# Attention of a hybrid decoder layer: keys requested ahead of the last group norm, the last head four slots later, value buffers laid over the keys; feed-forward: second half of the norm, splits and residual loads in another order

## The chip, the core and the metric

The kernel runs on one core of one Trainium2 chip. The metric is device time in microseconds (us), the median of several executions. TensorE (PE in the profile) multiplies matrices, VectorE (DVE) and ScalarE (ACT) work on elements, GpSimd (POOL) does little here, and SyncE (SP) issues most transfers. Each engine executes its own instructions in the order written for it, and waits on semaphores for the others.

## The reference

One layer of a decoder is computed for a prompt of 1024 tokens and for 8 sample tokens, 1032 columns in all. All data are float32.

```python
xn = rmsnorm(x, w)                                  # the same for the three mixers
sc_b, sc_c, sc_x, z, xbc, dt, q, gates = split(xn @ w_in)
y_a = (sc_b * conv3(sc_c * sc_x)) @ w_sc_out        # gated short convolution
y_b = group_rmsnorm(ssd(conv4(xbc), dt) * silu(z)) @ w_ssm_out   # Mamba-2, 32 heads, 4 groups
probs = softmax(q @ mem_k * 256 ** -0.5)            # 4 heads of 256, 256 memory tokens
y_c = (probs @ mem_v) @ w_attn_o
g_a, g_b, g_c = split(sigmoid(gates))
x = x + (g_a * y_a + g_b * y_b + g_c * y_c) @ w_merge_o
x = x + (silu(rmsnorm(x) @ w_gate) * (rmsnorm(x) @ w_up)) @ w_down   # hidden width 2816
y = rmsnorm(x)
```

The prompt's keys and values come from its memory tokens; each of the 8 sample rows has cached keys and values of its own. The outputs also hold new convolution and recurrent states.

## The kernel before

Activations lie transposed: 128 channels of a block on the partitions, 1032 tokens along the free axis. Every float32 operand of a matmul is split into a high and a low half (a copy on ScalarE, a subtraction on VectorE), and a product is made of three matmuls: high by high, high by low, low by high. In the names, a last `h` or `l` is a half, `r` a raw load.

`gemm` (L200) makes 128 rows of an output from 8 blocks of input, 3 halves and 512 + 256 + 264 columns, so 72 matmuls. Between the blocks it calls `tick()`, which runs the next piece of the list `pend`. The side work stands in that list: scan pieces during the input projections, attention pieces during the second output projection. `pace` is the length of the list over the number of matrices left, so the pieces are spread evenly, and a piece that is moved or removed shifts those behind it.

The stages in the order of time: norm and input projections; the scan's pieces between the gate products and the first output projection (`wo00` to `wo07`); the second output projection, whose 16 blocks of input come in two halves (`wo10` to `wo17`, `wo20` to `wo27`), with the attention pieces between its matmuls; `wo30` to `wo37` for the attention's output; the merge (`pm`, L1855) with the sum of squares for the second norm; the feed-forward part, whose products go by one level of Strassen's scheme; the final norm.

The attention pieces (list `pieces`, L1717): load the prompt's keys `kk` (`k_load`, L1553, onto SP), turn them on TensorE (`k_turn`, `pskT`, L1567) and split them into `kTh`, `kTl` (L1569, L1570); load a head's queries `qT` (`a_load`, L1665) and split them into `q00h` and so on; scores per 256 tokens (`a_scores`, `psa`, L1679), softmax (L1597 to L1606, `mx`, `pr`), turned probabilities (`a_probs`, `psp`, `pTh`, `pTl`), products with the values (`a_out`, `psv`, L1711). Beside them run the sample's rows `b` from 0 to 7: broadcast query `qb` (one buffer), cached keys `kc` (two buffers), scores on VectorE (L1588), and in the end one softmax and per row `s_values` (loads `vc`, in the buffers of `kc`) and `s_out` (`pso`, L1638, sixteen matmuls, eight for each half of the memory). Score tiles share two PSUM buffers. While `wo17` runs, the eight blocks of the second half are loaded (`in`, L1443, onto SP) and split into `b00` to `b07`.

In the last scan group, `group_norm` writes its four normed blocks to `yb_d` (L1198, onto SP). The keys and queries stand behind these on SP's queue.

The feed-forward part: `st_early` (L272) makes the first half of six products while the second half of the norm is not there yet; `norm_half` (psf L1804, psr L1817) makes the inverse root from the sums of squares `sq` (L1867) and spreads it. `strassen` (L311) makes four outputs out of seven products of 24 matmuls, called `B11`, `T1`, `nT2`, `B21`, `T3`, `B22`, `T4` after their right operand, on three PSUM tiles `m0` to `m2`. `first` evacuates a product (L319); in the down projection, `d00` to `d16`, it adds to the residual `x` in place (`into`). `used` runs a refill: after a product has used a right operand, the splits for the next half of the hidden blocks (`h0T30l` and so on, L1961). `tc.issue_after(i)` makes the scheduler place what follows behind instruction i on its engine. `residual` loads `x` again (L2004); `product` finishes the last hidden pair (L1980 to L1982).

Of the kernel before, what the change touches and what calls it, by code (L numbers as in the profile page):

```python
# [9 lines left out]
F32 = mybir.dt.float32  # L10
F32R = mybir.dt.float32r
# [6 lines left out]
P = 128  # L18
# [29 lines left out]
def tile_kernel(ctx: ExitStack, tc, a, o):  # L48
# [185 lines left out]
    pst = [None]  # L234
    freed = [None]
    count = [0]

# [33 lines left out]

    def st_early(blocks, forms):  # L272


        for first in range(0, len(blocks), 3):
            held = []
            for i, (src1, nm, out, keep) in enumerate(blocks[first : first + 3]):
                wA = st_split(st_raw(src1, f"{nm}Er"), f"{nm}E")
                ps = st_ps(f"m{i}", f"{nm}e")
                o1 = out()  # L280
                st_prod(forms, ps, wA, 0, "B11", True)
                S.copy(o1[:, HS[1]], hv(ps))
                held.append((wA, ps, o1, keep))
            for wA, ps, o1, keep in held:
                st_prod(forms, ps, wA, 512, "B21", False)
                S.copy(o1[:, HS[0]], hv(ps))
                keep(o1)
# [23 lines left out]
    def strassen(  # L311
# [5 lines left out]
        def first(dst, ps):  # L317
            if into:
                V.tensor_tensor(dst, ps, dst, op=ALU.add)  # L319
            else:  # L320
                S.copy(dst, ps)

        def used(f):
            turning.append(refill(f) if refill is not None else None)
            if len(turning) > LATE:
                g = turning.popleft()
                if g is not None:
                    g()

# [46 lines left out]
        if early is None:  # L376
            first(o12, hv(pa))
            used("nT2")
            prod(pc, wA, 512, "B21", True)
            V.tensor_tensor(o11, hv(pc), o11, op=ALU.add)  # L380
            used("B21")
        else:
            S.copy(o21, o12)
            V.tensor_sub(o22, o22, o12)
            freed[0] = V.tensor_tensor(o12, hv(pa), o12, op=ALU.add).ins
        if ready is None:
# [1110 lines left out]
    for i, (src, w) in enumerate(ins[:3]):  # L1497
# [5 lines left out]
            for m in range(KD)  # L1503
        )
    for g in range(GROUPS):
        xg, bcg, hold = groups[g]
# [5 lines left out]
        pend.extend(pieces[-3:])  # L1512
        pend.extend(z_pieces(g, xg, hold) + [None] + group_norm(g, xg, hold))
    pace[:] = len(pend) / (len(fillers) + KD) + 1e-6, 0.0
# [28 lines left out]
    if True:  # L1543
        kTh = at.tile([P, KD, MEM], F32R, tag="kTh", bufs=1, name="kTh")
        kTl = at.tile([P, KD, MEM], F32R, tag="kTl", bufs=1, name="kTl")
        vh = at.tile([P, 2, D], F32R, tag="vh", bufs=1, name="vh")
        vl = at.tile([P, 2, D], F32R, tag="vl", bufs=1, name="vl")
        sc_s = tri[:, 64:].rearrange("p (m b h) -> p m b h", m=2, b=NS)
        pTs = qs.rearrange("p t b -> p (t b)").rearrange("p (m c) -> p m c", m=2)

        kks = {}

        def k_load(m):  # L1553
            kks[m] = ev_tile(f"kk{m}", (P, D))
            SY.dma_start(kks[m], k_d[m])

# [70 lines left out]

        def s_values(b):
            for m in range(2):
                kcs[b, m] = at.tile([P, D], F32, tag="kc", name=f"vc{b}{m}")  # L1630
                SY.dma_start(kcs[b, m], a["cache_mem_v"][0, b, m * P : (m + 1) * P].rearrange("m h d -> m (h d)"))

        def s_out(b):
# [9 lines left out]
            S.copy(t, ps[:, :256])  # L1643
            if b + 1 < NS:
                s_values(b + 1)
            for h in range(AH):
# [56 lines left out]
        def a_out(h, dk):  # L1703
# [13 lines left out]
        pieces = [  # L1717
            [(k_load, 0), (k_load, 1), (a_load, 0)],
            [(k_turn, 0, 0)],
# [3 lines left out]
        for h in range(AH):  # L1723
# [3 lines left out]
            if h + 1 < AH:  # L1727
                pieces.append([(a_load, h + 1)])
            pieces.append([(a_out, h, 0)])
            pieces.append([(a_out, h, 1)])  # L1730
            if h == 2:
                pieces.extend([] for _ in range(4))
        pieces[5].append((k_turn, 1, 1))
        pieces[6].append((v_in, 1))
        for b in range(NS):
            at_ = 3 + 5 * b
            for i, fs in enumerate(
# [8 lines left out]
        pieces = [lambda fs=fs: run(fs) for fs in pieces]  # L1746
        pieces += [s_softmax, lambda: s_values(0), s_probs, None]
        for b in range(NS):
            pieces += [lambda b=b: s_out(b), None]
        pend.extend(pieces)  # L1750
        pend.extend(states)
        pend.extend([None, s_back])
        pace[:] = len(pend) / (len(outs) - 1) + 1e-6, 0.0
# [88 lines left out]
    for half in range(2):  # L1842
# [30 lines left out]
        else:  # L1873
            flush()
            norm_half(1, sq)
    aux_stack.close()
# [14 lines left out]
    for i, (nm, j) in enumerate((("g", 0), ("u", 0), ("g", 2), ("u", 2), ("g", 4), ("u", 4))):  # L1891
# [10 lines left out]
        )  # L1902
    st_early(blocks, forms)
    for kt in range(4):
# [100 lines left out]

    residual(0, 1, 2, 3)

    def opening():
        product()
        residual(4, 5, 6, 7)  # L2010

    for ch in range(2):
        for m in range(0, KD, 2):
# [3 lines left out]
                lambda m=m: (x2[m][:, HS[0]], x2[m][:, HS[1]], x2[m + 1][:, HS[0]], x2[m + 1][:, HS[1]]),  # L2017
                into=True, hook=opening if ch == 0 and m == 0 else None, **turn,
            )
# [134 lines left out]
```

## Time and profile before

| | us |
|---|---|
| median of 3 executions | 2461.08 (2458.73 to 2466.34) |
| the profiled execution | 2456.66 |
| its span, first to last instruction | 2454.6 |
| TensorE busy | 2425.3 (99%) |
| VectorE busy | 1582.8 (64%) |
| ScalarE busy | 1065.7 (43%) |
| mean granted TensorE clock | 0.997 |

A row of the waits names the waiting engine and the line, what ended the wait, the time in total, how often and the longest. A row of the timeline gives start, duration, engine, line, operation, output and inputs, and in brackets the idle time before it and what ended it; several alike are joined (x3). A row of the stretches gives from and to, the length, busy time by engine, the granted clock (1.00 is full speed), the share of the transfer engines and GB/s. [...]

### The profile page before, as it was taken

How to read it: one execution, taken by the hardware profiler on the slowest of the kernel's cores; microseconds unless marked ns; L12 is line 12 of the kernel's file. 1: busy time of each engine (PE TensorE's matmuls, PEld its weight loads, DVE VectorE, ACT ScalarE, POOL GpSimd, SP SyncE). 2: the span in 40 equal slices, each digit the busy share in tenths (PEclk: the TensorE clock that was granted, in tenths of full speed). 3: DMA queues.
4: the chain of work that ended last, by engine and by line, in shares of the span. 5: the costliest groups of instructions: out<-in, count | busy, mean ns of one | idle time of the engine just before them, and what ended most of it. 6: DMA issues, size and time to landing. Idle time of an engine off the chain costs nothing.

```text
span 2454.6 us, 45661 instructions
## 1 busy us (share of the span) xinstructions
PE 2425.3 (99%) x18946; PEld 2309.6 (94%) x18946; DVE 1582.8 (64%) x2591; ACT 1065.7 (43%) x1707; POOL 121.0 (5%) x163
## 2 busy tenths in 40 slices
PE   9999999999999999999999999999999999999998
PEld 7999999999999999888888887899999999999998
DVE  6854677777676774657767662555787555476756
ACT  6554455453545536456445441223443333342322
POOL 0200000000000001121120000000000000000000
PEclk9999999999999999999999999999999999999999
DMA  6445344354344456667867686865443323264421
GB/s 199 134 127 172 120 131 130 107 158 117 112 122 146 138 151 217 200 203 258 273 215 274 212 286 228 297 198 168 147 161 130 113 82 115 76 234 137 149 86 70
DMA packets 358622, 404.35 MB, mean 165 GB/s; under 512 B 16406, under 2 KB 285830, under 8 KB 358407
## 3 DMA queue, kind: packets, MB, share of 16 engines
q1 hardware_dynamic: 337966, 343.72, 44.9%
q10 hardware_dynamic: 20449, 57.71, 6.1%
q8 instruction: 149, 2.44, 0.4%
q14 instruction: 58, 0.48, 0.1%
HBM read 286.31 MB, written 115.29 MB: 164 GB/s over the span
## 4 chain that ended last, share of the span: by engine, by line
PE 88%; DVE 5%; DMA 4%; ACT 2%; issue 1%; SPq 0%; POOL 0%; ACTq 0%; DVEq 0%
PE po L220 13%; PE ps_q L220 4%; PE pm L1855 3%; PE ps_g L220 2%; PE pd L220 1%; PE py L1058 1%; PE pss L1071 1%; PE ps_z L220 1%; PE po L1050 1%; PE Z6m L266 1%; PE Z2m L266 1%; PE Z8m L266 1%; PE C3m L266 1%; PE Z14m L266 1%; PE C6m L266 1%
## 5 line engine op out<-in xcount | busy, mean ns | idle before, releaser
L1003 ACT ACTIVATE r<-r,acum 128x128 f32<-128x128 f32 x256 | 79.2, 392 | 4.6 <-DMA r<-ac_d 4.2
L774 DVE SCALAR_TENSOR_TENSOR ax<-u,prm,ax 128x1024 f32<-128x1024 f32 x44 | 56.4, 1281 | 0.3 <-ACT ax L771 0.2
L1035 POOL TENSOR_TENSOR xdd<-xdt,decst 128x512 f32<-128x512 f32 x32 | 37.0, 1157 | 293.1 <-DVE xdt L1031 293.1
L944 ACT ACTIVATE st<-st,es 128x128 f32<-128x128 f32 x128 | 41.5, 392 | 23.0 <-DMA st<-in_state_ssm_dram 17.6
L1054 DVE TENSOR_TENSOR y<-po,ea 128x512 f32<-128x512 f32 x28 | 19.3, 690 | 39.9 <-PE po L1050 37.1
L1490 DVE TENSOR_TENSOR yr<-po,yr 128x1032 f32<-128x1032 f32 x8 | 9.9, 1232 | 54.4 <-PE po L220 53.7
L946 DVE SCALAR_TENSOR_TENSOR st<-sr,dts,st 128x128 f32<-128x128 f32 x128 | 40.9, 354 | 0.4
L1029 DVE TENSOR_TENSOR r<-r,cbm 128x1024 f32<-128x1024 f32 x32 | 39.2, 1225 | 2.8 <-ACT bT L1028 0.5
L950 DVE SCALAR_TENSOR_TENSOR sr<-st,sr 128x128 f32<-128x128 f32 x128 | 36.1, 293 | 1.1
L1028 ACT COPY bT<-bp 128x128 f32<-128x128 f32 x32 | 8.5, 264 | 64.9 <-DVE cbm L1026 64.8
L2089 ACT ACTIVATE fj<-psy 128x512 f32<-128x512 f32 (+1 forms) x18 | 10.7, 596 | 58.3 <-PE psy L2087 58.2
L1071 PE MATMUL pss<-xdd,bT 128*128 128x512 f32 x64 | 33.4, 604 | 2.5 <-ACT bT L1028 2.5
L1058 PE MATMUL py<-r,xdt 128*64 128x128 f32 x512 | 35.0, 279 | 0.0
L1004 ACT ACTIVATE r<-r 128x1024 f32<-128x1024 f32 x32 | 33.8, 1058 | 0.7
L1031 DVE TENSOR_TENSOR xdt<-xp,dtT 128x512 f32<-128x512 f32 x32 | 21.9, 686 | 18.7 <-PE xp L1024 18.5
L1862 DVE TENSOR_TENSOR x<-pm,xT 128x516 f32<-128x516 f32 x16 | 11.1, 696 | 35.1 <-PE pm L1855 35.1
L1084 POOL TENSOR_TENSOR s<-s,cdec 128x512 f32<-128x512 f32 x28 | 32.0, 1143 | 4.8 <-DVE s L1077 4.5
L1058 PEld LDWEIGHTS py<-r,xdt 128*64 128x64 f32 x512 | 27.3, 136 | 4.2 <-issue 0.5
L1050 PE MATMUL po<-bc,s 128*128 128x128 f32 x224 | 29.8, 276 | 0.0
L1784 DVE TENSOR_TENSOR gt<-po,gt 128x1032 f32<-128x1032 f32 x8 | 9.9, 1232 | 29.8 <-PE po L220 29.2
L1588 DVE SCALAR_TENSOR_TENSOR kc<-kc,qb 128x256 f32<-128x256 f32 x64 | 23.5, 421 | 7.9 <-DMA qb<-qs_d 7.1
L777 DVE SCALAR_TENSOR_TENSOR ax<-u,prm,ax 128x1032 f32<-128x1032 f32 x22 | 28.4, 1290 | 0.0
(9065 smaller groups left out, 9063.0 us busy)
## 6 DMA issues: line engine op xcount, KB each, us to landing
r<-ac_d SPq DMA_DIRECT2D x32, 512.0 KB
gt<-gt_d SPq DMA_DIRECT2D x24, 516.0 KB
xs_d<-ax ACTq DMA_DIRECT2D x22, 516.0 KB
gt_d<-G ACTq DMA_DIRECT2D x20, 516.0 KB
x<-xs_d SPq DMA_DIRECT2D x16, 516.0 KB
zs<-zs_d SPq DMA_DIRECT2D x16, 516.0 KB
yb_d<-x SPq DMA_DIRECT2D x16, 516.0 KB
in<-yb_d SPq DMA_DIRECT2D x16, 516.0 KB
```

Of the source, the lines that this page charges most:

```text
L220: PE.matmul(out[:, c : c + n], wt[:, ks], x[:, c : c + n], start=(k == 0 and i == 0), stop=(k == nk - 1 and i == 2),)
L266: PE.matmul(hv(ps)[:, c : c + n], wt[:, ks], x[:, c : c + n], start=(start and kt == 0 and i == 0), stop=(kt == 3 and i == 2), skip_group_ ...
L774: V.scalar_tensor_tensor(acc[:, :T], u[:, j : j + T], w[j], acc[:, :T], op0=ALU.mult, op1=ALU.add)
L944: S.activation(st[:, i], st[:, i], AF.Copy, scale=es[:, g * 4 + i, b : b + 1])
L946: V.scalar_tensor_tensor(st[:, i], rb, dts[:, g * 4 + i, b : b + 1], st[:, i], op0=ALU.mult, op1=ALU.add)
L1003: S.activation(r[:, j, :], r[:, j, :], AF.Relu, scale=-1.0, bias=acum[:, c, h : h + 1])
L1029: V.tensor_tensor(r, r, bc(cbm.unsqueeze(1), [P, HPG, P]), op=ALU.mult)
L1035: G.tensor_tensor(b3(xdd, HPG), b3(xdt, HPG), bc(decst[:, c, hs].unsqueeze(2), [P, HPG, 64]), op=ALU.mult)
L1050: PE.matmul(po[:, t * P : (t + 1) * P], state["s"][:, t * P : (t + 1) * P], bcg[1][:, cs], start=True, stop=True,)
L1058: PE.matmul(py[hp : hp + 64, (h // 2) * P : (h // 2 + 1) * P], xdt[:, h * 64 : (h + 1) * 64], r[:, (h % 2) * 4 + h // 2, :], start=True, s ...
L1071: PE.matmul(pss, bT, xdd, start=True, stop=True)
L1855: PE.matmul(hv(ps)[:, c : c + n], wt[:, ks], x[:, half * HT + c : half * HT + c + n], start=(k == 0 and i == 0), stop=(k == KD - 1 and i = ...
```

## The change

1. The two key loads leave the first attention piece. They become a piece of their own just ahead of the last group's `group_norm`, and use activation buffers (tags `ah`, `al`) instead of `ev` buffers.
2. `kTh` and `kTl` get a pool of their own, which is closed at the second row of values. A pool of four value buffers is opened over it. Rows 0, 3 and 6 use the two old buffers, the others the four new ones. `s_out(b)` requests the values of row b + 3 instead of b + 1.
3. Behind head 2 stand eight slots instead of four, with the last conv state, the sample's softmax and its turned probabilities in them. The other conv states go along with `a_load`; before, all four stood at the end of the list. The sample's rows follow each other every four pieces instead of five. The list has 71 entries instead of 73, so the pace goes from 4.87 to 4.73 pieces a matrix.
4. `norm_half(1, sq)` moves from ahead of the early products to behind the first of them.
5. In `strassen`, the refill's splits are placed behind the last splits of weights and behind the last evacuation (`out[0]`).
6. The residual loads: blocks 0 and 1 first, 2 and 3 with `product`, 4 to 7 with the second pair of outputs. Before, 0 to 3 first and 4 to 7 with `product`.

```diff
+    out = [None]
...
-    def st_early(blocks, forms):
+    def st_early(blocks, forms, then):
...
                 st_prod(forms, ps, wA, 0, "B11", True)
                 S.copy(o1[:, HS[1]], hv(ps))
                 held.append((wA, ps, o1, keep))
+                if first + i == 0:
+                    then()
...
             if into:
-                V.tensor_tensor(dst, ps, dst, op=ALU.add)
+                out[0] = V.tensor_tensor(dst, ps, dst, op=ALU.add).ins
...
                 if g is not None:
-                    g()
+                    with tc.issue_after(prev["hi"]), tc.issue_after(prev["lo"]), tc.issue_after(out[0]):
+                        g()
...
-            freed[0] = V.tensor_tensor(o12, hv(pa), o12, op=ALU.add).ins
+            freed[0] = out[0] = V.tensor_tensor(o12, hv(pa), o12, op=ALU.add).ins
...
+    def k_load(m):
+        kks[m] = act_tile(("ah", "al")[m], f"kk{m}", F32)[:, :D]
+        SY.dma_start(kks[m], k_d[m])
...
-        pend.extend(z_pieces(g, xg, hold) + [None] + group_norm(g, xg, hold))
+        pend.extend(z_pieces(g, xg, hold) + [None])
+        if g == GROUPS - 1:
+            pend.append(lambda: [k_load(m) for m in range(2)])
+        pend.extend(group_norm(g, xg, hold))
...
-        kTh = at.tile([P, KD, MEM], F32R, tag="kTh", bufs=1, name="kTh")
-        kTl = at.tile([P, KD, MEM], F32R, tag="kTl", bufs=1, name="kTl")
...
+        akt = ExitStack()
+        keys = akt.enter_context(tc.tile_pool(name="akt", bufs=1, reuse_waits="tile"))
+        kTh = keys.tile([P, KD, MEM], F32R, tag="kTh", name="kTh")
+        kTl = keys.tile([P, KD, MEM], F32R, tag="kTl", name="kTl")
+        vcp = []
...
         def s_values(b):
+            if b == 1:
+                akt.close()
+                vcp.append(att_stack.enter_context(tc.tile_pool(name="avc", bufs=4, reuse_waits="tile")))
             for m in range(2):
-                kcs[b, m] = at.tile([P, D], F32, tag="kc", name=f"vc{b}{m}")
+                po = vcp[0] if b % 3 else at
+                kcs[b, m] = po.tile([P, D], F32, tag="kc", name=f"vc{b}{m}")
...
-            if b + 1 < NS:
-                s_values(b + 1)
+            if b + 3 < NS:
+                s_values(b + 3)
...
-            [(k_load, 0), (k_load, 1), (a_load, 0)],
+            [(a_load, 0)],
...
             if h + 1 < AH:
-                pieces.append([(a_load, h + 1)])
+                pieces.append([(a_load, h + 1), (states[h],)])
...
             if h == 2:
-                pieces.extend([] for _ in range(4))
+                pieces.extend([[(states[3],)], [], [(s_softmax,)], [(s_probs,)], [], [], [], []])
+                last = len(pieces)
...
+        for b, i in enumerate((1, 4, 6)):
+            pieces[last + i].append((s_values, b))
         for b in range(NS):
-            at_ = 3 + 5 * b
+            at_ = 3 + 4 * b
...
-        pieces += [s_softmax, lambda: s_values(0), s_probs, None]
...
-        pend.extend(states)
-        pend.extend([None, s_back])
+        pend.extend([None] * 3 + [s_back])
...
             flush()
-            norm_half(1, sq)
...
-    st_early(blocks, forms)
+    st_early(blocks, forms, lambda: norm_half(1, sq))
...
-    residual(0, 1, 2, 3)
+    residual(0, 1)
...
         product()
-        residual(4, 5, 6, 7)
-
+        residual(2, 3)
+
+    hooks = [opening, lambda: residual(4, 5, 6, 7)]
...
-                into=True, hook=opening if ch == 0 and m == 0 else None, **turn,
+                into=True, hook=hooks.pop(0) if hooks else None, **turn,
```

On SP before, around the key loads (`kk0`, `kk1`); `qs_d` are the sample's queries, `qT00` and `qT01` the first head's:

```order
L1198 DMA yb_d_122<-x33_13773 128x1032
L1209 DMA qs_d_141<-qrows_14691 8x1024
L1555 DMA kk0_14731<-k_d_136 128x1024
L1555 DMA kk1_14733<-k_d_136 128x1024
L1665 DMA qT00_14735<-q_d_135 128x1032
```

and the same loads in the change, among the loads of `wo10`'s input blocks (`in02` to `in05`):

```order
L1447 DMA in02_14564<-yb_d_122 128x1032
L1447 DMA in03_14579<-yb_d_122 128x1032
L1513 DMA kk0_14581<-k_d_136 128x1024
L1513 DMA kk1_14583<-k_d_136 128x1024
L1447 DMA in04_14598<-yb_d_122 128x1032
```

The keys have passed four `in` loads and the four `yb_d` stores.

On TensorE before, the last block of `wo11` and the first scores (`psa0_0`):

```order
L220 MATMUL po11_14858<-b07l_14723,wo11h_14854 128x264
L1567 MATMUL pskT10_14791<-ident_75,kk1_14733 128x128 x4
L1567 MATMUL pskT01_14816<-ident_75,kk0_14731 128x128 x4
L220 MATMUL po11_14858<-b07h_14722,wo11l_14855 128x512
L220 MATMUL po11_14858<-b07h_14722,wo11l_14855 128x256
L220 MATMUL po11_14858<-b07h_14722,wo11l_14855 128x264
L1679 MATMUL psa0_0_14859<-kTh_14712,q00h_14737 128x256
L1680 MATMUL psa0_0_14859<-kTl_14713,q00h_14737 128x256
```

and in the change, where the first scores stand in the seventh of `wo11`'s eight blocks:

```order
L220 MATMUL po11_14865<-b06h_14729,wo11h_14861 128x264
L1695 MATMUL psa0_0_14866<-kTh_14725,q00h_14744 128x256
L1696 MATMUL psa0_0_14866<-kTl_14726,q00h_14744 128x256
L1695 MATMUL psa0_1_14899<-kTh_14725,q00h_14744 128x256
L1696 MATMUL psa0_1_14899<-kTl_14726,q00h_14744 128x256
L220 MATMUL po11_14865<-b06l_14730,wo11h_14861 128x512
```

The turns (`pskT`) have gone up into `wo10`, and the scores stand ahead of the five last groups of three matmuls of `wo11`.

On VectorE before, the first evacuations of the down projection (`x3_0`, `x3_1` out of `d00m0`, `d00m1`) among the refill's splits:

```order
L1961 TENSOR_TENSOR h0B220l_23856<-h0B220l_23856,h0B220h_23855 128x2x516
L1961 TENSOR_TENSOR h0B221l_23858<-h0B221l_23858,h0B221h_23857 128x2x516
L319 TENSOR_TENSOR x3_0_23903<-d00m0_23914,x3_0_23903 128x516
L1961 TENSOR_TENSOR h0T40l_23894<-h0T40l_23894,h0T40h_23893 128x2x516
L319 TENSOR_TENSOR x3_1_23905<-d00m1_23915,x3_1_23905 128x516
L1961 TENSOR_TENSOR h0T41l_23896<-h0T41l_23896,h0T41h_23895 128x2x516
```

and in the change:

```order
L322 TENSOR_TENSOR x3_0_23915<-d00m0_23922,x3_0_23915 128x516
L1977 TENSOR_TENSOR h0T30l_23833<-h0T30l_23833,h0T30h_23832 128x2x516
L1977 TENSOR_TENSOR h0T31l_23835<-h0T31l_23835,h0T31h_23834 128x2x516
L322 TENSOR_TENSOR x3_1_23917<-d00m1_23923,x3_1_23917 128x516
L1977 TENSOR_TENSOR h0B220l_23868<-h0B220l_23868,h0B220h_23867 128x2x516
L1977 TENSOR_TENSOR h0B221l_23870<-h0B221l_23870,h0B221h_23869 128x2x516
```

The first evacuation now precedes the splits of `T3` and `B22`, the second those of `B22` and `T4`.

More of the change, by code (lines that the diff above doesn't have):

```diff
@@ L1504, in tile_kernel @@
         )
+    kks = {}
+    def k_load(m):
+        kks[m] = act_tile(("ah", "al")[m], f"kk{m}", F32)[:, :D]
+        SY.dma_start(kks[m], k_d[m])
     for g in range(GROUPS):
@@ L1543, in tile_kernel @@
     if True:
-        kTh = at.tile([P, KD, MEM], F32R, tag="kTh", bufs=1, name="kTh")
-        kTl = at.tile([P, KD, MEM], F32R, tag="kTl", bufs=1, name="kTl")
         vh = at.tile([P, 2, D], F32R, tag="vh", bufs=1, name="vh")
         vl = at.tile([P, 2, D], F32R, tag="vl", bufs=1, name="vl")
+        for tag, shape, bufs in (("qb", [P, D], 1), ("kc", [P, D], 2), ("mx", [P, 4], 2), ("pr", [P, 2, MEM], 3)):
+            at.tile(shape, F32, tag=tag, bufs=bufs, name=tag + "_")
+        akt = ExitStack()
[3 more added lines that the diff above has]
+        vcp = []
         sc_s = tri[:, 64:].rearrange("p (m b h) -> p m b h", m=2, b=NS)
         pTs = qs.rearrange("p t b -> p (t b)").rearrange("p (m c) -> p m c", m=2)
[L1551 to L1555, printed above, removed]
         def v_in(m):
```

## The prediction

> **What bounds the kernel now.** I read the page first, then TensorE's waits, then the timeline around the longest of them, and last the granted clock by stretches. The page gives the busy time by engine:
>
> ```profile
> PE 2425.3 (99%) x18946; PEld 2309.6 (94%) x18946; DVE 1582.8 (64%) x2591; ACT 1065.7 (43%) x1707; POOL 121.0 (5%) x163
> ```
>
> TensorE is busy for all but 29.3 us of the 2454.6 us span. So an edit pays only where it shortens one of TensorE's waits, lowers the time of a matmul, or lets matmuls follow each other more closely. The waits, with what ended them, the total, the count and the longest:
>
> ```profile
> PE psa L1679 <- DVE kTl L1570: 2.1, 1, 2.1
> PE psa L1679 <- ACT pr L1600: 1.8, 1, 1.8
> ...
> PE d00m L266 <- DVE x L319: 1.2, 1, 1.2
> ...
> PE psf L1804 <- DVE sq L1867: 0.9, 1, 0.9
> ...
> PE d02m L266 <- DVE d02Al L254: 0.4, 1, 0.4
> ```
>
> Together 6.4 us, each once. That alone would be under 0.3% of the time. But a wait has a second price here. The stretches below give from:to, length, busy time of PE, PEld, DVE, ACT and POOL, then the granted clock:
>
> ```profile
> 1334.00:1341.00 7.00, 6.93 (x39) 6.55 (x40) 5.21 (x7) 4.69 (x6) 0.00 (x0) 0.76 0.86 278
> 1336.00:1338.60 2.60, 2.60 (x12) 2.40 (x12) 1.94 (x2) 1.31 (x2) 0.00 (x0) 0.50 1.00 297
> 1454.00:1461.00 7.00, 6.57 (x39) 6.33 (x40) 4.82 (x15) 3.17 (x12) 0.00 (x0) 0.76 1.04 358
> 1755.00:1761.00 6.00, 6.00 (x40) 6.00 (x39) 3.46 (x9) 2.06 (x6) 0.00 (x0) 0.72 0.10 31
> 2202.00:2209.00 7.00, 5.60 (x45) 5.18 (x44) 7.00 (x9) 0.62 (x1) 0.00 (x0) 1.00 1.04 408
> ```
>
> Right behind the key wait (2.1), head 3's wait (1.8) and the norm's wait (0.9) the clock drops to half: at 0.76 over 7.00 us, 0.24 x 7.00 = 1.7 us of work is lost, and 0.28 x 6.00 = 1.7 in the third. The wait of 1.2 in the down projection is followed by full clock. So the three places that the first four parts of the change touch hold 2.1 + 1.8 + 0.9 = 4.8 us of waits and 3 x 1.7 = 5.1 us of halved clock.
>
> **The change part by part.** *Keys earlier.* The wait at the first scores, with the steps behind it:
>
> ```profile
> 1334.07 0.36 PE L1679 MATMUL psa<-kTh,q00h 128*128 128x256 f32 x1 [2.07 <-DVE kTl L1570]
> ```
> ```profile
> 1296.69 5.40 SPq L1443 DMA_DIRECT2D in<-yb_d  x3
> ...
> 1321.42 1.22 SPq L1555 DMA_DIRECT2D kk<-k_d  x2
> 1322.73 0.99 SPq L1665 DMA_DIRECT2D qT<-q_d  x2
> ```
> ```profile
> 1324.17 1.05 ACT L168 CAST wo13h<-wo13r 128x1024 fp32r<-128x1024 f32 x1 [5.83 <-PE po L220]
> ```
> ```profile
> 1333.23 0.69 DVE L1570 TENSOR_TENSOR kTl<-pskT,kTh 128x512 fp32r<-128x512 f32 x1
> ```
>
> The key loads stand on SP behind the four yb_d stores and are issued at 1321.42; their turns and splits then come one by one until 1333.9. In the new order they go ahead of the third of the `in` loads at 1296.69, so by 1302.1 at the latest, some 20 us earlier; the first two turns lie in wo10's sixth block, and the three subtractions stand on VectorE ahead of wo13l. Two things move against it. The four `in` loads behind the keys come two loads later. And TensorE comes to the first scores sooner: they stand now ahead of five groups of three po matmuls (0.47 each, below) that ran before them, so at 1334.07 - 2.07 - 5 x 0.47 = 1329.6. What is late next is q00h: qT still goes out after the stores, and its cast stands third behind wo10's last matmul, after wo13h and wo10's evacuation. That matmul is where 1324.17 stands, plus 1 to 2 us of turns that now precede it; three copies of about 1.05 later it is 1328.3 to 1329.3. So 0 to 1 us may stay if qT lands late; I take 0.3. The loads of wo14 and wo15 slide behind the stores; their casts are wanted a whole matrix later, which hides it. Gain 2.1 + 1.7 - 0.3 = 3.5; if q00h is late by over about a microsecond, the halved clock stays too and the gain is near 1.
>
> *Last head four slots later.* Head 3's third score tile needed a buffer that the exponentials of the first had not left:
>
> ```profile
> 1453.36 0.47 ACT L1600 ACTIVATE pr<-psa,mx 128x256 f32<-128x256 f32 x1 [0.74 <-DVE mx L1598]
> ```
> ```profile
> 1431.27 15.12 SPq L1443 DMA_DIRECT2D in<-yb_d  x8
> ```
> ```profile
> 1443.40 1.23 DVE L179 TENSOR_TENSOR b01l<-in,b01h 128x1032 fp32r<-128x1032 f32 x1 [1.33 <-ACT b01h L178]
> ...
> 1453.97 1.23 DVE L179 TENSOR_TENSOR b07l<-in,b07h 128x1032 fp32r<-128x1032 f32 x1
> ```
> ```profile
> 1446.43 0.63 PE L220 MATMUL po<-b00h,wo20h 128*128 128x512 f32 x3
> ```
>
> VectorE and ScalarE were splitting b01 to b07 (1443.4 to 1455.2) at that moment. Four slots are nearly a matrix of wo2x, so the scores start when the splits are over: gain 1.8 + 1.7 = 3.5. The price lies on SP: two value loads now stand ahead of the eight `in` loads and wait until VectorE has finished row 7's scores. I place the `in` issue some 14 us before wo20 instead of 15.2 (1431.27 against wo20's start at 1446.4). A block is nine such matmuls, 3 x 0.47 = 1.41 us: b01 is wanted at 1447.8 and there at 1444.6, 3.2 us to spare; b07 is wanted at 1456.3 and there at 1455.2, of which some 2 us are the softmax that leaves. So 3 us of cover for each, and I cost a delay of 1 to 2 us at nothing; each microsecond beyond 3 is one of waiting.
>
> *Queries every four slots.* They have one query buffer, and VectorE waits on it already:
>
> ```profile
> DVE kc L1588 <- DMA qb<-qs_d: 7.1, 4, 2.2
> ```
>
> Closer requests put these waits ahead of probability subtractions that heads 1 and 2 need. From nothing (hidden, as the four are now) to the 2.2 us of the longest, twice; I take 1.2, since most fall where TensorE has matmuls of wo1x to run.
>
> *Values asked three rows ahead.* Of the value products, the first row shows two halves together, the second one half by itself between po matmuls:
>
> ```profile
> 1490.65 1.07 PE L1638 MATMUL pso<-vc,qs 128*32 128x256 f32 x16
> 1491.65 0.73 PE L220 MATMUL po<-b04h,wo22h 128*128 128x512 f32 x3
> 1492.22 0.64 PE L220 MATMUL po<-b04l,wo22h 128*128 128x512 f32 x3
> ```
> ```profile
> 1511.23 0.62 PE L220 MATMUL po<-b07l,wo23h 128*128 128x512 f32 x3
> 1511.70 0.40 PE L220 MATMUL po<-b07h,wo23l 128*128 128x512 f32 x1
> 1512.02 0.64 PE L1638 MATMUL pso<-vc,qs 128*32 128x256 f32 x8
> 1512.59 0.50 PE L220 MATMUL po<-b07h,wo23l 128*128 128x256 f32 x2
> 1512.93 0.64 PE L220 MATMUL po<-b00h,wo24h 128*128 128x512 f32 x3
> ```
>
> Three po matmuls take 0.47 us (1511.23 to 1511.70). Together, both halves cost 1492.22 - 1490.65 - 0.47 = 1.10 us. Alone, one costs 1512.93 - 1511.70 - 0.47 = 0.76, two 1.52. Six of the eight rows are cut so now and none in the new order: 6 x 0.42, of which I take 2.4. With more buffers no load holds up the product.
>
> *Norm's second half.* The sum of squares was asked for before it was ready:
>
> ```profile
> 1753.08 1.50 PE L1804 MATMUL psf<-ones,sq 128*128 128x1 f32 x12 [0.92 <-DVE sq L1867]
> ```
>
> It moves behind the eight matmuls that end g0e (45 such take 5.60 us in the stretch from 2202, 0.124 each), so 1.0 us, which covers the 0.9; psr then has twelve of u0e between, 1.5 us for the chain of small steps on the root. Gain 0.9 + 1.7, less 0.1: 2.5.
>
> *Splits and residual loads in the down projection.* The evacuation that d00m waits for, and the loads in front of d02's weight:
>
> ```profile
> 2203.60 0.69 DVE L319 TENSOR_TENSOR x<-d00m,x 128x516 f32<-128x516 f32 x1
> ```
> ```profile
> 2201.79 6.95 SPq L2004 DMA_DIRECT2D x<-x_d  x4
> 2208.84 3.02 SPq L245 DMA_DIRECT2D d02r<-in_w_ffn_down_dram  x4
> ```
>
> The evacuation now stands before the splits of T3, B22 and T4, and d02's loads pass the last four residual loads, which take 6.95 us to go out, so they can go some 6 us earlier, while d02's first products stand one product (24 matmuls of 0.124, 3 us) earlier. The splits come later by an evacuation or two (0.69 each) and have over 3 us until TensorE reads them. Waits of 1.2 + 0.4 go: 1.6.
>
> The sum: 3.5 + 3.5 + 2.4 + 2.5 + 1.6 - 1.2 = 12.3 us, which against the profiled execution of 2456.66 us gives 2444.4. The median of the runs is 4.4 above that execution, so 2461.1 - 12.3 = 2448.8.
>
> [...]
>
> **The rivals.** *The halved clock has another cause.* Then the waits go and the slow stretches stay or turn up elsewhere: 12.3 - 5.1 leaves a gain of 7.2, 2453.9. For it: the 1.2 us wait at 2203 was followed by 1.00. Against it: three slow stretches, each just behind one of the three waits. Chance 0.12.
>
> *New waits in the attention stage.* A query load in front of VectorE's subtractions, or an `in` load at wo20, stops TensorE for 1 to 2 us, and the clock halves behind it. Two such cost 2 x (1.5 + 1.7) = 6.4, 1.2 of it counted already: gain 7.1, three leave 4: 2454 to 2457. For it: the four query waits above, the one query buffer; against it: none of them stops TensorE now. Chance 0.16.
>
> *The change does not do what it says for the keys.* They take activation buffers, and if those come free only with wo10's blocks, or if q00h comes last anyway, the wait stays: gain 8.8, 2452.3. Against it: the `in` loads beside them, on the same buffers, were out by 1302.1. Chance 0.06.
>
> *Slower: the value loads hold the queue.* They wait for row 7's scores, which wait for a query load, with all eight `in` loads of wo2x behind. Each microsecond beyond the 3 us of cover is a wait at wo20's blocks. It decides from 3 + 12.3 = 15 us late, and is slower by more than 0.3% from some 23 us. The longest wait of that chain now is the 2.2 us above, so only a stack of them, or a buffer held until a later stage, comes there. At 23 us: 2468.5. Chance 0.04.
>
> **How the numbers follow.** The forecast has 0.62 and gives 2448.8, by itself 2444 to 2454: a gain of 13.9 with nothing left of the waits and no new one, 7.4 with the two query waits of 2.2 and a halved clock behind one, and 2 to 3 us of the runs' own spread (2458.73 lies 2.4 under their median). A measurement of this kernel can tell 0.3%, 7.4 us: faster means under 2453.7. Range: 2443 to 2458, which takes in the first three rivals and leaves the last, and the ends, out. Faster: 0.62 + 0.06 + half of 0.12 + a third of 0.16 = 0.79; same: the other half and most of the rest, 0.16; slower: 0.04 and 0.01 for four or more new waits, 0.05.
>
> **What would show it.** Right: the first psa no longer waits for kTl, or under 1 us; no wait for pr at wo20; psf's wait under 0.2; pso in groups of sixteen; d00m's wait for x gone; the clock at 1.00 in all three stretches; TensorE idle near 23 us. Wrong: clock 0.50 without a wait before it (the first rival), a new wait of psp, psv or po for pTl, kc or b0x (the second), psa waiting for q00h (the third), SP's `in` loads starting later than 13 us before wo20 (the last), or T3, B22 or T4 late for d00m.

## The result, and the profile after

The changed kernel takes 2456.91 us (median of 13 executions, 2451.11 to 2458.68) where the kernel before takes 2460.60 in 13: the ratio is 0.998, its 95% interval 0.9973 to 0.9988. That is 3.7 us faster, inside 0.3%; 12.3 us had been forecast. The profiled execution took 2455.26 us, with a span of 2453.3 us.

```profile
PE 2424.7 (99%) x18946; PEld 2313.5 (94%) x18946; DVE 1583.8 (65%) x2591; ACT 1067.3 (44%) x1707; POOL 124.2 (5%) x163
```

TensorE is idle for 28.6 us of it, where 29.3 were idle before and about 23 were forecast. Its waits, longest first, with the rows that the argument needs:

```profile
PE pss_pT L1637 <- DVE prs L1618: 5.7, 1, 5.7
...
PE psp L1709 <- DVE pTl L1717: 1.0, 1, 1.0
...
PE po L220 <- DVE b03l L179: 0.5, 1, 0.5
PE po L220 <- DVE b05l L179: 0.5, 1, 0.5
PE d00m L267 <- DVE x L322: 0.4, 1, 0.4
```

The waits that the change was aimed at are gone: no psa for kTl (2.1 before), none for pr (1.8), none of psf for sq (0.9), and d00m waits 0.4 instead of 1.2. At the top stands one that did not exist, 5.7 us at the turn of the sample's probabilities. The stretches show the granted clock (behind POOL's column) at the first scores, in wo20, at the norm and at the first product of the down projection:

```profile
1329.00:1336.00 7.00, 7.00 (x53) 6.61 (x52) 3.11 (x4) 3.05 (x3) 0.00 (x0) 1.00 1.00 322
1451.30:1458.10 6.80, 6.42 (x23) 5.78 (x24) 4.06 (x5) 3.06 (x4) 0.00 (x0) 0.50 0.91 296
1752.00:1760.00 8.00, 8.00 (x69) 7.83 (x68) 3.91 (x9) 3.11 (x6) 0.00 (x0) 1.00 0.33 105
2200.00:2207.00 7.00, 6.57 (x56) 6.36 (x55) 5.92 (x8) 2.81 (x3) 0.00 (x0) 1.00 1.03 412
```

The clock is full at the keys and at the norm, as forecast. It is at half for the 6.80 us that begin just before the new wait ends; TensorE works in 6.42 of them. Its timeline at that place:

```profile
1445.62 0.39 PE L220 MATMUL po<-b01l,wo20h 128*128 128x512 f32 x1
1451.68 0.42 PE L1637 MATMUL pss_pT<-ident,prs 32*128 32x32 f32 x2 [5.67 <-DVE prs L1618]
1452.03 0.80 PE L220 MATMUL po<-b01l,wo20h 128*128 128x256 f32 x2
1452.63 1.06 PE L220 MATMUL po<-b01h,wo20l 128*128 128x512 f32 x3
1453.49 1.06 PE L220 MATMUL po<-b02h,wo20h 128*128 128x512 f32 x3
...
1458.42 0.64 PE L220 MATMUL po<-b04h,wo20h 128*128 128x512 f32 x3
1458.89 0.64 PE L220 MATMUL po<-b04l,wo20h 128*128 128x512 f32 x3
```

Two little turns, of 32 x 32, stand between matmuls of wo20's second block, and hold up all that is behind them. Groups of three po matmuls start 0.86 us apart behind the wait and 0.47 apart from 1458.42 on, so at half clock they start 1.8 times as far apart, not quite twice, which by estimate costs about 6.42 x (0.86 - 0.47) / 0.86 = 2.9 us here. What VectorE does meanwhile:

```profile
1447.13 1.23 DVE L179 TENSOR_TENSOR b03l<-in,b03h 128x1032 fp32r<-128x1032 f32 x1 [3.19 <-ACT b03h L178]
1448.28 0.41 DVE L1609 TENSOR_REDUCE mxs<-pss_sc 32x1 f32<-32x256 f32 x1
1448.67 1.23 DVE L179 TENSOR_TENSOR b04l<-in,b04h 128x1032 fp32r<-128x1032 f32 x1
1449.83 0.13 DVE L1610 TENSOR_SCALAR mxs<-mxs 32x1 f32<-32x1 f32 x1
1449.95 1.23 DVE L179 TENSOR_TENSOR b05l<-in,b05h 128x1032 fp32r<-128x1032 f32 x1
1451.10 0.14 DVE L1616 RECIPROCAL mxs<-mxs 32x1 f32<-32x1 f32 x1
1451.28 0.34 DVE L1618 TENSOR_SCALAR prs<-prs,mxs 32x256 f32<-32x256 f32 x1
```

The four steps of the sample's softmax (mxs, mxs, mxs, prs) stand one by one among and behind the splits of b03 to b05. VectorE meets them in that order, and before the first it waits 3.19 us for b03h. The softmax's own work is 0.41 + 0.13 + 0.14 + 0.34 = 1.0 us. The reason for the wait lies on SP, whose rows give the issue of each load:

```profile
1428.88 1.71 SPq L1647 DMA_DIRECT2D vc<-in_cache_mem_v_dram  x2
1430.68 1.45 SPq L1447 DMA_DIRECT2D in<-yb_d  x3
1432.77 0.38 SPq L140 DMA_DIRECT2D wo24r<-in_w_ssm_out_dram  x1
1440.41 6.84 SPq L1447 DMA_DIRECT2D in<-yb_d  x5
```

Three of the `in` loads go out together, the fourth only at 1440.41, ten microseconds behind the first; it brings b03. SP's waits from 1430 to 1445 say for what:

```profile
SPq L1447 <- DMA in<-yb_d: 4.9, 1, 4.9
SPq L1447 <- DMA at_d<-ot: 3.3, 1, 3.3
SPq L1447 <- DVE b00l L179: 2.3, 1, 2.3
```

The fourth load takes the buffer of the first: it waits until that has landed (4.9) and until VectorE has made b00l out of it (2.3, to 1440.39). The wait of 3.3 is the fifth load's, for head 2's output. ScalarE's timeline says why that output is stored so late:

```profile
1438.06 1.05 ACT L178 CAST b00h<-in 128x1032 fp32r<-128x1032 f32 x1 [5.13 <-DMA in<-yb_d]
1438.12 0.33 ACTq L1731 DMA_DIRECT2D at_d<-ot  x1
...
1446.05 1.05 ACT L178 CAST b03h<-in 128x1032 fp32r<-128x1032 f32 x1 [3.37 <-DMA in<-yb_d]
```

Head 2's output is stored from ScalarE's queue, behind the cast of b00, which waits for the first `in` load. The fifth `in` load wants the buffer of that output, so it waits for a store that waits for a load. In the kernel before, the fourth load goes out at 1440.22, after 7.2 us of waiting for the same output; but there the store is issued ahead of the cast of b00 and only its landing is late:

```profile
1431.68 0.36 ACTq L1715 DMA_DIRECT2D at_d<-ot  x1
...
1439.75 1.05 ACT L178 CAST b00h<-in 128x1032 fp32r<-128x1032 f32 x1 [4.34 <-DMA in<-yb_d]
```

What stands among the splits of that kernel is head 3's softmax, and TensorE waits 1.8 us for it, the wait that the change was to remove:

```profile
1450.22 1.23 DVE L179 TENSOR_TENSOR b05l<-in,b05h 128x1032 fp32r<-128x1032 f32 x1
1451.36 0.69 DVE L1597 TENSOR_REDUCE mx<-psa 128x2 f32<-128x512 f32 x1
1451.96 1.22 DVE L179 TENSOR_TENSOR b06l<-in,b06h 128x1032 fp32r<-128x1032 f32 x1
```

So the change took one softmax out from among the splits and put another in, two blocks earlier among them; and the fourth load goes out 3.3 us ahead of wo20 (1440.41 against 1443.74) where it was 6.2 (1440.22 against 1446.43).

In time, by stretches of TensorE from the start of one product to the start of another, in the profiled executions before and after and in one of the kernel with the softmax moved (experiment 4):

| from, to | before | after | softmax among the last scores |
|---|---|---|---|
| wo10's second block, wo14 | 73.4 | 68.1 | 68.8 |
| wo14, wo30 | 185.1 | 189.1 | 183.7 |
| wo30, g0e | 184.7 | 185.9 | 184.5 |
| g0e, first pair | 39.0 | 36.5 | 36.5 |
| first pair, d00 | 405.6 | 407.2 | 407.2 |
| d00, last matmul | 252.1 | 249.4 | 249.8 |
| all of it | 1139.9 | 1136.2 | 1130.4 |

From wo14 to wo30 lie the last head, the queries and the values, where the forecast has 3.5 - 1.2 + 2.4 = 4.7 us to gain; 4.0 are lost, with the wait and the halved clock, 5.7 + 2.9 = 8.6, in them. The 1.2 from wo30 to g0e are not explained; of the 1.6 from the first pair to d00, 1.1 are in the hidden products (last section). Ahead of wo10's second block, where the change adds little but the key loads, the second execution is 2.4 us longer (1309.24 against 1306.86), with two halved stretches (0.50 for 3.41 us each, from 55.25 and 1123.62 us) that the first has not.

### The profile page after: what moved, and what is told of

Its sections match the earlier page's. It is cut to its first block, busy times and chain, and to the rows that moved or that the text cites. A ratio compares the mean times of both kernels' runs of the same rounds, so it can differ in the third digit from the quotient of the medians.

```text
span 2453.3 us, 45655 instructions
## 1 busy us (share of the span) xinstructions
PE 2424.7 (99%) x18946; PEld 2313.5 (94%) x18946; DVE 1583.8 (65%) x2591; ACT 1067.3 (44%) x1707; POOL 124.2 (5%) x163
## 4 chain that ended last, share of the span: by engine, by line
PE 89%; DVE 4%; DMA 4%; ACT 1%; issue 1%; SPq 0%; POOL 0%; DVEq 0%; ACTq 0%
PE po L220 12%; PE ps_q L220 4%; PE pm L1872 3%; PE ps_g L220 2%; PE pd L220 1%; PE py L1062 1%; PE pss L1075 1%; PE ps_z L220 1%; PE po L1054 1%; PE Z6m L267 1%; PE Z2m L267 1%; PE C4m L267 1%; PE d02m L267 1%; PE G8m L267 1%; PE u20m L267 1%
## 5 line engine op out<-in xcount | busy, mean ns | idle before, releaser
L1058 DVE TENSOR_TENSOR y<-po,ea 128x512 f32<-128x512 f32 x28 | 19.3, 690 | 38.7 <-PE po L1054 36.6
L1033 DVE TENSOR_TENSOR r<-r,cbm 128x1024 f32<-128x1024 f32 x32 | 39.2, 1224 | 2.7 <-ACT bT L1032 0.5
L1075 PE MATMUL pss<-xdd,bT 128*128 128x512 f32 x64 | 33.6, 606 | 0.8 <-ACT bT L1032 0.8
L1054 PEld LDWEIGHTS po<-bc,s 128*128 128x128 f32 x224 | 27.7, 191 | 0.8 <-DVE s L1081 0.2
```

What stands on the lines that cost most here:

```text
L1033: V.tensor_tensor(r, r, bc(cbm.unsqueeze(1), [P, HPG, P]), op=ALU.mult)
L1054: PE.matmul(po[:, t * P : (t + 1) * P], state["s"][:, t * P : (t + 1) * P], bcg[1][:, cs], start=True, stop=True,)
L1075: PE.matmul(pss, bT, xdd, start=True, stop=True)
```

## The experiments

All ratios are to the kernel before on the same chip, with a 95% interval.

**1. The softmax four slots later.**

```diff
-                pieces.extend([[(states[3],)], [], [(s_softmax,)], [(s_probs,)], [], [], [], []])
+                pieces.extend([[(states[3],)], [], [], [], [], [], [(s_softmax,)], [(s_probs,)]])
```

> The changed kernel with the sample's softmax and its turned probabilities four slots later in the gap behind head 2 (slots 7 and 8 of the eight instead of 3 and 4); nothing else. Theory: what ate the gain is one wait, 5.7 us of TensorE at the turn of the sample's probabilities (pss_pT), whose normalisation stands on VectorE among the splits of b03 to b05 that wait for their loads, and two windows of halved clock behind it, 3.4 us. With the softmax behind the splits the wait falls to 0 to 2 us and the clock stays full: 2448 to 2451 us where the changed kernel has 2456.9, ratio to before 0.995 to 0.996. Rival: the splits wait for late loads whatever stands among them, and TensorE then waits for b03 to b07 instead: 3 to 5 us of wait, one or two halved windows, 2454 to 2457. Second rival: the halved clock falls into the same stretch without a wait.

Measured: 2453.79 us, ratio 0.9967 (0.9955 to 0.9979). On VectorE the softmax now stands behind b07's split, and the turn in wo20's seventh block. VectorE is still busy with the splits when TensorE comes to the turn:

```profile
PE pss_pT L1637 <- DVE prs L1618: 4.2, 1, 4.2
```

Faster than the changed kernel, by ratio, by some 3 us and not by 6 or more: the move took 1.5 us off the wait and one halved stretch of two (groups of three po matmuls start 0.86 us apart from 1455.76 to 1458.34 alone). So it doesn't tell the theories apart: the wait was not taken away.

**2. The softmax behind all heads**, as before the change.

```diff
+                pieces.extend([[(states[3],)], [], [], [], [], [], [], []])
...
+        pieces += [s_softmax, None, s_probs, None]
```

> The changed kernel with the sample's softmax and probabilities behind all heads, ahead of the value products, as the kernel before had them. Theory: no wait at pss_pT. But in this order head 3's scores stand in wo20, among the splits of b03 to b07, as before the change, so its own wait (1.8 us and one halved window) may come back: 2449 to 2454. Rival (loads late whatever stands there): waits for b03 to b07 of 3 to 5 us, 2454 to 2457.

Measured: 2453.33 us, ratio 0.9967 (0.9956 to 0.9979). No wait at pss_pT; but the list has four entries more, the pace rises, and every piece lands elsewhere. New waits came in the first heads:

```profile
PE psv L1727 <- DVE pTl L1717: 2.0, 1, 2.0
PE psp L1709 <- DVE pr L1618: 1.5, 1, 1.5
```

So the length of the list was a second thing changed; the next runs that move the softmax keep it.

**3. The softmax beside the last head's value products, and 4. among its scores.** Both have the eight slots behind head 2 with only the last conv state in them.

```diff
+        pieces[last + 6].append((s_softmax,))
+        pieces[last + 7].append((s_probs,))
```
```diff
+        pieces[last + 2].append((s_softmax,))
+        pieces[last + 4].append((s_probs,))
```

> The changed kernel with the sample's softmax and its turned probabilities beside the last head's two value products (the seventh and eighth of that head's nine slots), so behind all splits of b00 to b07 with two slots to spare; the list keeps its length. Theory: no wait at pss_pT over 0.5 us, none for b03 to b07 over 1 us in sum, no halved window between wo20 and wo22: 5 to 6 us of wait and 1.7 to 3.4 us of halved clock less than the changed kernel, 2447 to 2451 us, ratio to before 0.9945 to 0.9965. Rival (the late loads cost the same wherever the softmax stands): waits of 3 us or more for b03 to b07, 2452 to 2456.

> As the run beside it, but with the softmax and the probabilities among the last head's scores (its third and fifth slot). Theory: VectorE meets them only after b07's split, so there is no wait at pss_pT over 1 us; they share the two score tiles in PSUM with the head's scores, which may cost 0 to 1 us there: 2447 to 2452 us, ratio 0.9945 to 0.997. Rival: 2452 to 2456.

Measured: 2451.66 us, ratio 0.997 (0.9959 to 0.9982), and 2451.82 us, ratio 0.9971 (0.9959 to 0.9983). The second was run again with the changed kernel itself on one chip:

> The kernel with the softmax among the last head's scores once more, beside the next two and the kernel before on one chip. Theory: with the wait gone, parts two and three give about 4 us over the kernel without them (head 3's wait of 2 to 3 us and some 2 us of joined value products, less 1 to 2 us of new waits): ratio to before 0.995 to 0.997, 3 to 5 us below the next. Rival: they give nothing even so, and the two are equal within 2 us.

> The changed kernel itself on the same chip. Theory: the wait of 5 to 6 us at pss_pT stands in it again, with one or two halved windows; ratio 0.9975 to 0.999, 5 to 8 us above the kernel with the softmax in the last head and 1 to 4 above the one without heads and values. Rival: the wait is an accident of the one profiled execution, and the time is that of the kernel with the softmax moved.

Measured: 2450.75 us (2448.20 to 2451.61, 5 runs), ratio 0.9962 (0.9948 to 0.9975), against 2455.28 us (2453.02 to 2458.79, 12 runs), ratio 0.998 (0.9971 to 0.999). Each of the five is below each of the twelve. The wait was no accident of one execution; the changed kernel's second profile has

```profile
PE pss_pT L1637 <- DVE prs L1618: 6.9, 1, 6.9
```

and the kernel with the softmax among the last scores has these, and a full clock from 1440 to 1480 us:

```profile
PE psa L1695 <- ACT pr L1612: 1.2, 2, 0.8
...
PE psp L1709 <- DVE pTl L1717: 1.0, 1, 1.0
...
PE po L220 <- DVE b03l L179: 0.7, 2, 0.5
PE po L220 <- DVE b04l L179: 0.5, 1, 0.5
```
```profile
1440.00:1480.00 40.00, 38.10 (x250) 33.86 (x250) 23.36 (x42) 17.72 (x35) 0.00 (x0) 1.00 0.85 296
```

Its `in` loads are no earlier (the fourth goes out 11 us behind the first), and po waits 1.2 us for them in all. The rival that the loads cost the same wherever the softmax stands, with waits of 3 us or more for b03 to b07, is refuted: what cost more was a piece on TensorE's path placed among the work that waits for them.

The price is less than the sum of wait and halved clock. From wo20's first product to wo22's first, TensorE does the same products in the changed kernel as here, but for two little matmuls (pss_sc) that fall in here too; it needs 38.7 and 39.2 us in the changed kernel's two profiles, 33.6 and 32.9 in the two of this kernel. That is 5 to 6 us, not 8.6, since without the long wait TensorE meets shorter ones there (1.9 us of idleness in the 33.6); the rest is not taken apart. In the medians on one chip it is 4.5. On that chip this kernel is the fastest of the four compared there, about 9 us below the kernel before. By ratio its first run, 0.9971, is level with experiments 1, 2, 3 and 8.

**5. The keys alone.** Part 1 of the change on the kernel before.

```diff
+        if g == GROUPS - 1:
+            pend.append(lambda: [k_load(m) for m in range(2)])
...
-            [(k_load, 0), (k_load, 1), (a_load, 0)],
+            [(a_load, 0)],
```

> The kernel before with the earlier key loads alone. Theory: the wait of the first scores falls from 2.1 to under 1 us and the halved window behind it goes: 3.5 us faster than before by the stretch from wo10 to wo14, ratio 0.998 to 0.9995. Rival (the halved clock has another cause): the stretch gains 1.5 to 2 us, and a halved window stays in it.

Measured: 2457.49 us, ratio 0.9987 (0.9977 to 0.9997). The first scores do not wait; from wo10's second block to wo14's first it is 4.4 us shorter (73.4 before, 69.0), 2.3 more than the wait. But the halved stretch at head 3, which nothing had touched, is gone too: the wait is still there, 2.1 us long, and the clock behind it is full (1.00):

```profile
PE psa L1682 <- ACT pr L1603: 2.4, 2, 2.1
```
```profile
1447.00:1455.00 8.00, 5.62 (x40) 4.83 (x40) 6.64 (x18) 4.05 (x14) 0.00 (x0) 1.00 1.02 331
```

**6. The norm alone.** Part 4 on the kernel before.

```diff
-            norm_half(1, sq)
...
+    st_early(blocks, forms, lambda: norm_half(1, sq))
```

> The kernel before with the second half of the norm behind the first early product alone. Theory: the wait of 0.9 us at psf goes and no halved window begins within 4 us of it: 0.9 to 2.6 us faster in the stretch from g0e to the first pair, ratio 0.9985 to 0.9998. Rival (the halved window has another cause): a halved window stays between 1750 and 1765.

Measured: 2459.74 us, ratio 0.9997 (0.9986 to 1.0008). The wait at psf and the halved stretch behind it are gone in the profile (the clock is 1.00 from 1748 to 1756 us), where the stretch from g0e to the first pair is 2.5 us shorter; the time does not show it. Here both the key wait and head 3's stand untouched, and neither is followed by half clock (1.00 in the 10 and 11 us around them):

```profile
PE psa L1681 <- ACT pr L1602: 2.1, 2, 1.8
PE psa L1681 <- DVE kTl L1572: 2.1, 1, 2.1
```
```profile
1328.00:1338.00 10.00, 7.93 (x57) 7.11 (x56) 7.69 (x10) 7.41 (x9) 0.00 (x0) 1.00 0.67 235
1447.00:1458.00 11.00, 8.86 (x62) 7.83 (x61) 9.42 (x21) 7.16 (x18) 0.00 (x0) 1.00 0.90 292
```

**7. The down projection alone.** Parts 5 and 6 on the kernel before.

```diff
+                    with tc.issue_after(prev["hi"]), tc.issue_after(prev["lo"]), tc.issue_after(out[0]):
+                        g()
...
+    hooks = [opening, lambda: residual(4, 5, 6, 7)]
```

> The kernel before with the new order of the refill's splits and of the residual loads alone. Theory: the waits of 1.2 us at the first nT2 and 0.4 us at d02 go, those at d06 to d14 change by under 1 us in sum: 1.5 to 3 us faster between the first product of the down projection and its end, ratio 0.9985 to 1.0. Rival: the splits of T3, B22 and T4 come too late and the same time is waited for there, ratio 1.0.

Measured: 2456.15 us, ratio 0.998 (0.997 to 0.9989). From the first product to the final norm's projection it is 2.8 us shorter in the profile (199.5 before, 196.7). The medians differ by 5.4, with an interval of about 2.7 to 7.4, so the profile's 2.8 lies at its lower end; what more there is was not traced. The waits at d02 and d06 are gone, a new one of 0.8 stands at d12, and d00m still waits 0.6 for x.

**8. Without the heads and the values.** Parts 1, 4, 5 and 6 together on the kernel before.

> The kernel before with the earlier keys, the moved second half of the norm, the order of splits and residual loads; without the later last head, the value buffers and the closer queries. Theory: this holds the keys' 2, the norm's 0.9 and the down projection's 2 to 3 us of waits, and on average half of the halved windows that followed them; head 3's wait of about 2 us stays: 5 to 8 us faster than before, 2453 to 2456, ratio 0.9965 to 0.998, so about as fast as the changed kernel, whose two other parts then gave nothing. Rival: parts two and three pay by themselves as forecast (about 6 us), and this kernel is slower than the changed one by 2 us or more: 2459 and above.

> The kernel with the keys, the norm and the down projection alone once more. Theory: ratio 0.9965 to 0.998, 3 to 5 us above the kernel with the softmax in the last head. Rival: equal to it within 2 us.

Measured: 2451.57 us, ratio 0.9968 (0.9956 to 0.9981), and 2452.59 us, ratio 0.9972 (0.9961 to 0.9983). Head 3's wait is 3.3 us in the first and 4.0 in the second:

```profile
PE psa L1686 <- ACT pr L1607: 4.0, 1, 4.0
```

On one chip this kernel lies 2.7 us below the changed one (2452.59 against 2455.28) and 1.8 above the one with the softmax among the last scores (2450.75). So parts 2 and 3 as written took back some of what the others gave. Whether they pay once the softmax is moved isn't settled: the pair of medians on the other chip (2451.82 for the softmax among the last scores, 2451.57 here) shows no difference, and 3 to 5 us had been expected.

**9. Waits of chosen length.** The kernel with the softmax among the last scores, with idle copies behind nT2 in fourteen hidden products; what is computed stays the same.

```diff
+            if not into and nm[0] in "gu" and 6 <= int(nm[1:]) <= 18:
+                for _ in range(14 + 5 * len(probed) % 11):
+                    S.copy(tri, hv(pa)[:, :P])
+                probed.append(nm)
```

> The kernel with the softmax in the last head's slots, with 14 to 24 idle copies of 128x128 on ScalarE out of the product tile between nT2 and T3 of each of fourteen hidden products (g6 to u18), so that TensorE waits there for some 0.5 to 4 us; where no wait stood and the clock was full. What is computed stays the same. Theory from the runs so far: the clock is granted by fixed stretches of 3.413 us, and one in which TensorE idles for more than about half (1.80 us and more did, 1.73 and less did not) is followed by one at half clock. Then waits under 1.7 us never halve, waits over 3.4 always, those between according to how they lie across a boundary, and each halved stretch costs 1.7 us. Rival (the halved windows only happen to lie near waits): no relation to the idle share of the stretch before. [...]

Measured: 2470.93 us in one execution. The copies were shorter than assumed, and no wait passed 1.0 us:

```profile
PE g8m L267 <- ACT tri L385: 1.0, 1, 1.0
```
```profile
1880.00:2160.00 280.00, 268.56 (x2203) 263.48 (x2202) 141.98 (x183) 145.20 (x357) 0.00 (x0) 1.00 0.27 87
```

TensorE idles for 11.4 us in those 280, in waits of at most 1.0, and the clock is full throughout. That agrees with the lower half of the expectation; waits of 2 to 4 us were not made, so the length at which the clock drops stays untested by a wait made for it.

## Why the prediction was wrong

The waits that it named went nearly as it said. It overlooked one step of the change, put the parts in the attention stage too high, and took the halved clock of one execution for that of all. Point by point:

- **Keys, 3.5 us.** Right in the profile: the wait went, q00h was there in time, and the stretch from wo10 to wo14 is 4.4 us shorter in the kernel with the keys alone, 5.3 in the changed one. Not forecast: 1.1 us come back in the hidden products (last section).
- **Last head, 3.5 us.** Here is the step that failed. "Four slots are nearly a matrix of wo2x, so the scores start when the splits are over" held, and so did "I cost a delay of 1 to 2 us at nothing" for the scores and nearly for the blocks. But the same edit puts s_softmax and s_probs into the gap, and the prediction gave these no term. It reckoned what late `in` loads do to po, not what they do to a chain that stands among the splits on VectorE and ends in a turn on TensorE. In the profile that is a wait of 5.7 us and 2.9 of halved clock; moving the softmax away gives 5 to 6 us in the stretch and 4.5 in the medians. The changed kernel's order on VectorE shows mxs between the splits of b03 and b04, and it was there to be read.
- **The SP rival** was named for the loads (value loads ahead of `in`) and priced as slower from 15 us of delay on; the loads were late for another reason: the fourth takes the buffer of the first, the fifth that of head 2's output. The rival that came true is the second, new waits in the attention stage. Its time was 2454 to 2457 and 2456.9 the result, inside the range for this rival's sake; but it was one wait of 5.7 us, by a chain that the rival does not name, and not two of 1.5, so that the number fits is luck.
- **Queries every four slots, -1.2.** Right: psp waits 1.0 for pTl, whose subtraction stands on VectorE behind a wait of 2.3 us for a query (qb).
- **Values, 2.4.** All eight products stand as groups of sixteen. Not separated from the rest in time. With the softmax among the last scores, the stretch from wo14 to wo30 takes 183.7 and 182.7 us in two profiles, where the kernel before needs 185.1 with a halved stretch in it, and the kernels with the keys or the norm alone 183.8 and 184.3 with full clock (1.00) behind head 3's wait. So last head, values and queries together give some 1 to 2 us of the 4.7, and part of that is the clock.
- **Norm, 2.5.** Right in the profile (2.5 from g0e to the first pair), not visible in the time of the part alone.
- **Down projection, 1.6.** Mis-sized: 2.7 us from the first product to the final norm in the changed kernel, 2.8 in the part alone. The wait at d06 that was left uncounted went too.
- **Halved clock, 5.1 of the 12.3.** The second step that failed, by its size, since one execution was taken for all. In the profile before, all three waits, of 2.1, 1.8 and 0.9 us, happened to have a halved stretch behind them; in the kernels with the keys alone (2.1) and the norm alone (2.1 and 1.8) the waits left untouched at the keys and head 3 have full clock (1.00) behind them. Averaged over its 13 runs on the first chip the changed kernel's clock is 0.9956, over its 12 on the last 0.9955; the kernel before has 0.9960 on the last chip (19 runs), the kernel with the softmax among the last scores 0.9970 (5 runs). By the price below, the latter gains 2 us of clock on the kernel before and not 5.1, and the new wait loses the changed kernel what it had gained.

For the kernel without the new wait, the correction for the clock alone gives 12.3 - 5.1 + 2.2 = 9.4, where 8.9 was measured on the last chip; but there errors cancel: less from the last head, values and queries, and the hidden products, against more from the keys (5.3 where 3.5 was forecast) and the down projection (2.7 where it was 1.6). The changed kernel lies 4.5 above it, at 4.4 below the kernel before on that chip and 3.7 on the first.

## What to carry to other kernels

Where pieces are moved into a gap to keep one engine clear, follow each of them on every engine that it touches: a chain of 1 us of work that ends on the critical engine can hold it up for as long as all that stands between its links takes (5.7 us here). A single profile may hold waits whose second price is a matter of luck (here 1.8 to 2.1 us were followed by half clock in one profile and by full clock in two others); before counting it, look at the clock over several runs. And a part that is worth less than the spread of the runs should be measured by its stretch in the trace, with the rest of the program unchanged in length.

## What the runs showed of the hardware

- **The clock was at half for stretches of 3.41 us, most of them behind a wait of TensorE, and the length of the wait did not settle it.** Between 20 and 2440 us of the profile before, the clock is at 0.50 from 1335.38 to 1338.79, 1454.84 to 1458.26 and 1755.21 to 1758.63: 3.41 us each, and their starts lie 35 and 88 times 3.413 apart. In the 3.41 us ahead of each, TensorE is idle for 2.07, 1.84 and 0.92 us; behind the 0.92, the wait at psf, stand twelve matmuls of one column (1.50 us). But 1.22 us at d00m, from 2202.36 to 2205.77, are followed by full clock. In the changed kernel's first profile the clock is at 0.50 from 55.25 to 58.66, 1123.62 to 1127.03 and 1451.30 to 1458.12, the last twice 3.41. In the 3.41 us ahead of the first two, TensorE is idle for 0.39 and 0.00 us. Of the long wait, 1.88 us lie from 1444.47 to 1447.89, with full clock behind them; the 3.41 up to 1451.30 are idle throughout, with half clock behind them; and the 3.41 after that, themselves at half and with 0.38 us of idleness, are followed by another 3.41 at half. Of the waits left untouched in the kernels with the keys alone (2.1) and the norm alone (2.1 and 1.8), none is followed by half clock (1.00). The 0.92 and the 1.88 do not fit the theory that stands ahead of experiment 9 (1.80 and more, not 1.73 and less), and what decides was not shown.
- **The spread of the runs goes with the clock.** The kernel before, 27 executions on one chip, by their mean clock: 0.998 2455.4 us, 0.997 2458.3, 0.996 2461.1, 0.995 2462.6, 0.994 2464.2, so 2.2 us for 0.001. That is the larger part of the spread; at one clock, 0.996, eleven executions still lie between 2459.0 and 2463.6. One halved stretch is, as an estimate from its length, 0.5 x 3.413 / 2454.6 = 0.0007 of clock, and by po matmuls 0.86 us apart instead of 0.47 about 3.41 x 0.39 / 0.86 = 1.5 us.
- **Hidden products are 0.07 us longer each in the kernels with early keys** (20.01 and 19.93 us a product, 1.1 us from g6 to u20; the run with the idle copies can't be compared) and not in the three without, the kernel before and those with the norm or the down projection alone. No wait stands there. What differs isn't known, and nothing was tried on it.
